# Neighbour-sum kernel: windowed one-hots in pass 1, and half of the spread moved to TensorE and ScalarE

## The chip, the cores and the metric

The kernel runs on one core of one Trainium2 chip. The metric is the device time in microseconds (us), as a median of several executions. Each experiment was timed in alternation with the kernel before on the same chip. On two of the five chips used for experiments the kernel before itself took about 477 us instead of 368, at a lower mean granted clock (0.81 to 0.85 instead of 0.91 to 0.93; the clock granted to TensorE, as a share of full speed); comparisons of totals from those two are marked as disturbed and carry no verdict.

## The reference

```python
# 4096 nodes x 128 f32 features, 65536 edges, random src and dst
output = zeros((4096, 128))
for i in range(65536):
    output[dst[i]] += node_features[src[i]]
```

## The kernel before

Work goes through 128-edge tiles (T = 512). **Pass 1** sorts edges by destination block (32 blocks of 128 nodes). It has six quads q0 to q5, each with four slices of up to 22 tiles. For each quad VectorE builds a one-hot of the block (`oh1s`: for every edge a row with a single 1), TensorE and ScalarE count ranks from it (`counts`, which starts from VectorE's `scan`, the running totals of the tiles), and VectorE multiplies that one-hot by two payloads (`spread1`: the code of the edge, and its source block plus one). For each slice VectorE then builds a one-hot of the rank over 128 slots, and TensorE moves the payloads into their slots (`move1`), giving `sa` and `sbk`. From those come the gather keys, and with them the indices of rows that GpSimd gathers for output blocks 0 to 7 from a bf16 copy of the features (three parts whose sum is the f32 value). **Pass 2** makes the 24 remaining output blocks (slots 0 to 23) from 32 small matrices each; the stretch in which pass 1 has ended and pass 2's first group is being prepared is called the transition here. TensorE writes into PSUM buffers; tiles that take turns in the same buffers are said to share a ring.

The letters V, S, G and PE stand for VectorE, ScalarE, GpSimd (POOL in the profile) and TensorE.

```python
    p2b = [sb1.tile([P, NCH, P], BF16, name=f"p2b{i}") for i in range(2)]
    for t in p2b:                                    # prologue fills
        G.memset(t[:, :NH, 64:], 0.0)
        G.memset(t[:, NH:, :64], 0.0)
    # ... cut ...
    def x_part(i, v):                                # part v of features, quarter i
        part = x3[:, i * BX:(i + 1) * BX, v, :]
        S.activation(out=part, in_=xf[i][:], func=COPY, scale=-1.0)
        if v < 2:
            for h in range(2):
                bs = slice(h * BX // 2, (h + 1) * BX // 2)
                G.tensor_tensor(out=xf[i][:, bs], in0=xf[i][:, bs], in1=part[:, bs], op=OP.add)
        # ... else: the quarter is written to x3d, from which rows are gathered ...

    def counts(q):
        # ... for every four tiles: early/sums matmuls into psc (ring psA), then
            S.activation(out=cum[...], func=RELU, bias=minus[:], in_=psc[...])
            yield
        # ... psr = sum of cum over blocks; rank1[q] = copy of psr ...

    def spread1(q):
        v1[q] = sb2.tile([P, NL, 2, NB], BF16, name="v1", tag="t1")
        for k, key in ((0, kab), (1, kb[:])):
            V.tensor_tensor(out=v1[q][:, :, k, :]..., in0=oh1q(q)..., in1=key[:, q, ...], op=OP.mult)

    def move1(q, meanwhile=lambda i: None):
        psm = ps.tile([P, 512], F32, name="psm", tag="misc", bufs=1)
        for l in range(4):
            # ... p1 for two slices, n tiles in this slice ...
            onehot(p1[:, l % 2, :n], rank1[q][:, l, :n], n)         # all 128 slots
            meanwhile(l)
            for j in range(n):
                PE.matmul(out=psm[:, l * 64:(l + 1) * 64], lhsT=p1[:, l % 2, j, :],
                          rhs=v1[q][:, 4 * j + l].rearrange("p k b -> p (k b)"), ...)
        S.copy(out=sa[:, place(q), :], ...)
        S.copy(out=sbk[:, place(q), :], ...)
    # ... cut ...
    for q in range(NQ):
        move1(q, during(q))                          # during: pieces of count(q + 2), x parts
        if q + 3 < NQ:
            oh1s(q + 3)
        if q + 1 < NQ:
            spread1(q + 1)
        if q == 1:
            serve(0)                                 # gather keys and gathers
        if 1 <= q < NQ - 1:
            serve(q)
        if q + 3 < NQ:
            scan(q + 3)
        # ... add_up: matmuls of gathered rows ...
```

## Time and profile before

| | before |
|---|---|
| median | 367.97 us (367.55 to 368.44) |
| profiled span, mean granted TensorE clock | 366.4 us, 0.921 |
| busy TensorE / VectorE / ScalarE / GpSimd | 299.4 / 287.0 / 160.2 / 224.5 us |
| first permutation one-hot of q0 starts | 19.41 us |
| copy of `sa` starts, q0 to q5 | 37.65, 45.97, 58.12, 68.89, 77.01, 86.98 us |
| first gather | 49.19 us |
| first result of pass 2, last result | 146.17 us, 363.08 us |

A line of the timeline has the start and the length in us, the engine, the source line, the operation, the output and input with their sizes, and how many instructions the group holds. A bracket at its end says how long the engine had been idle and what released it. The start of the `sa` copy is used below as the end E of a quad, since nothing that follows from the quad can begin earlier.

### The profile page before, as it was taken

To read this page: it belongs to the slowest core of one execution; us is meant where nothing else is said; L and a number is where in the kernel's file an instruction comes from. 1 tells how busy PE (TensorE), PEld (TensorE's weight loads), DVE (VectorE), ACT (ScalarE), POOL (GpSimd) and SP (SyncE) were. 2 spreads that over 40 slices of the span, in tenths; PEclk is the share of its full clock that TensorE was granted. 3 is DMA by queue.
4 is the path that set the end of the run, shared out by engine and by line. 5 is a ranking of instruction groups with operands and counts; after the bars stand their busy time and mean duration, and the time that the engine had idled before them with its cause. 6 is when DMAs were issued, how large, how long until landed. Compare 5 with 4: busy or idle time off the path is not lost.

```text
span 366.4 us, 8352 instructions
## 1 busy us (share of the span) xinstructions
PE 299.4 (82%) x3527; PEld 219.8 (60%) x3527; DVE 287.0 (78%) x476; ACT 160.2 (44%) x297; POOL 224.5 (61%) x225
## 2 busy tenths in 40 slices
PE   0768867656373597979989999997799999999996
PEld 0557746535351466756667767675477676767663
DVE  4982899999759689699994799659994959687721
ACT  2778733300000373525534553545345555464650
POOL 5677048787877777706887768578437575775000
PEclk9978988978565699989999999999899999999999
DMA  8400922233232233310324323232213332332000
GB/s 245 114 2 2 311 74 73 69 73 79 62 79 77 75 80 81 91 29 13 82 64 99 87 75 75 64 86 67 70 36 85 72 86 72 90 85 71 26 9 21
DMA packets 22694, 27.96 MB, mean 76 GB/s; under 512 B 3776, under 2 KB 19328, under 8 KB 22656
## 3 DMA queue, kind: packets, MB, share of 16 engines
q0 software_dynamic: 9216, 18.89, 21.2%
q1 hardware_dynamic: 13296, 8.01, 7.6%
q8 instruction: 27, 0.44, 0.5%
q10 hardware_dynamic: 144, 0.52, 0.4%
q14 instruction: 11, 0.09, 0.1%
HBM read 22.02 MB, written 5.39 MB: 75 GB/s over the span
## 4 chain that ended last, share of the span: by engine, by line
PE 55%; DVE 36%; ACT 5%; DMA 1%; issue 1%; DVEq 0%
PE pso L530 27%; DVE oh L196 10%; PE psa L524 9%; DVE p L196 8%; PE psg L325 6%; PE ps L496 4%; DVE cum L465 3%; DVE v L257 3%; DVE oh L442 3%; PE psr L474 3%; PE psb L449 2%; ACT cum L236 2%; DVE v L456 2%; PE psr L241 1%; ACT x L178 1%; DVE cum L470 1%
## 5 line engine op out<-in xcount | busy, mean ns | idle before, releaser
L306 POOL DMA_INDIRECT rows<-x3d,gidx x192 | 199.8, 1041 | 101.2 <-issue 48.1
L530 PE MATMUL pso<-x,a 128*128 128x384 bf16 x768 | 156.3, 328 | 5.5 <-DVE res L333 5.5
L526 ACT CAST a<-psa 128x512 bf16<-128x512 f32 x192 | 112.1, 586 | 77.5 <-PE psa L524 77.0
L530 PEld LDWEIGHTS <-a 128*128 128x128 bf16 x768 | 67.8, 98 | 32.1 <-issue 6.5
L524 PE MATMUL psa<-oh 128*128 128x128 bf16 x768 | 74.3, 220 | 1.2 <-ACT a L526 0.9
L524 PEld LDWEIGHTS <-oh 128*128 128x128 bf16 x768 | 59.0, 98 | 26.1 <-issue 2.5
L196 DVE TENSOR_TENSOR oh<-psi,slo 128x4096 bf16<-128x4096 uint16 x24 | 54.7, 2281 | 10.0 <-PE psa L524 10.0
L196 DVE TENSOR_TENSOR oh<-psi,dlo 128x4096 bf16<-128x4096 uint16 x24 | 54.7, 2278 | 0.0
L325 PE MATMUL psg<-rows,ohg 128*128 128x384 bf16 x192 | 40.2, 353 | 4.5 <-DMA rows<-x3d,gidx 3.0
L196 DVE TENSOR_TENSOR p<-psi,rank 128x2688 bf16<-128x2688 uint16 (+1 forms) x24 | 36.1, 1566 | 0.0
L325 PEld LDWEIGHTS <-ohg 128*128 128x128 bf16 x192 | 19.0, 104 | 17.1 <-DVE ohg L196 4.7
L504 DVE TENSOR_SCALAR slo<-pa 128x128 uint16<-128x128 uint16 x12 | 3.0, 252 | 32.8 <-ACT pa L500 32.8
L236 ACT ACTIVATE cum<-psc,minus 128x512 bf16<-128x512 f32 (+1 forms) x36 | 22.0, 656 | 12.2 <-PE psc L233 11.8
L182 POOL TENSOR_TENSOR xf<-xf,x 128x512 f32<-128x512 f32 x16 | 19.8, 1275 | 11.3 <-ACT x L178 11.3
L196 DVE TENSOR_TENSOR p2b<-psi,rank 128x768 bf16<-128x768 uint16 x48 | 23.3, 545 | 2.3 <-ACT rank L479 2.3
L280 PE MATMUL psm<-v,p 128*128 128x64 bf16 x512 | 20.6, 200 | 4.9 <-DVE p L196 4.8
L449 PE MATMUL psb<-oh,before 128*128 128x128 bf16 (+1 forms) x96 | 12.3, 309 | 14.7 <-DVE oh L442 11.8
L280 PEld LDWEIGHTS <-p 128*128 128x128 bf16 x512 | 18.6, 103 | 6.9 <-DVE p L196 6.5
L496 PEld LDWEIGHTS <-p2b 128*128 128x128 bf16 x576 | 19.7, 101 | 3.6 <-DVE p2b L196 2.1
L333 DVE TENSOR_REDUCE res<-pso 128x128 f32<-128x384 f32 x24 | 13.1, 546 | 10.0 <-PE pso L530 10.0
L233 PEld LDWEIGHTS <-sums 128*128 128x128 bf16 x126 | 12.1, 116 | 14.4 <-issue 6.6
L449 PEld LDWEIGHTS <-before 128*128 128x128 bf16 x96 | 10.0, 127 | 17.2 <-DVE oh L442 12.7
(72 smaller groups left out, 255.2 us busy)
## 6 DMA issues: line engine op xcount, KB each, us to landing
x3d<-x SPq DMA_DIRECT2D x4, 768.0 KB, 4.8
rows<-x3d,gidx POOLq DMA_INDIRECT x192
xf<-in_node_features_dram SPq DMA_DIRECT2D x4, 512.0 KB, 7.9
out_dram<-res SPq DMA_DIRECT2D x32, 64.0 KB, 1.9
raw<-in_edge_index_src_dram ACTq DMA_DIRECT2D x1, 512.0 KB, 5.2
raw<-in_edge_index_dst_dram SPq DMA_DIRECT2D x1, 512.0 KB
x3d<-zrow SPq DMA_DIRECT2D x1, 96.0 KB, 5.7
x3d<-zrow SPq DMA_DIRECT2D x1, 48.0 KB
```

The costliest lines, as they stand in the source:

```text
L182: G.tensor_tensor(out=xf[i][:, bs], in0=xf[i][:, bs], in1=part[:, bs], op=OP.add)
L196: V.tensor_tensor(out=dst.rearrange("p i (m k) -> p i m k", k=2), in0=io.rearrange("p i (m k) -> p i m k", k=2), in1=keys2[:, :, None, :]. ...
L236: S.activation(out=cum[:, :, 4 * j0:4 * (j0 + n)], func=RELU, bias=minus[:], in_=psc[:, :n * P].rearrange("p (t b) -> p b t", b=NB))
L280: PE.matmul(out=psm[:, l * 64:(l + 1) * 64], lhsT=p1[:, l % 2, j, :], rhs=v1[q][:, 4 * j + l].rearrange("p k b -> p (k b)"), start=j == 0, ...
L306: G.indirect_dma_start(out=t[:, l, :], out_offset=None, in_=x3d[:, :], in_offset=bass.IndirectOffsetOnAxis(ap=gidx[:, place(q).start + l, ...
L325: PE.matmul(out=psg[d][:, :3 * P], lhsT=oh[:, l, :], rhs=t[:, l, :], start=q == 0 and l == 0, stop=q == NQ - 1 and l == 3)
L333: V.tensor_reduce(out=res[:], in_=pso[:, :3 * P].rearrange("p (v f) -> p f v", v=3), op=OP.add, axis=AX.X, negate=True)
L449: PE.matmul(out=psb[:, h * W:(h + 1) * W], lhsT=before[:], rhs=flat2(oh2)[:, h * NH + c], start=c == 0, stop=c == NH - 1)
L496: PE.matmul(out=ps2[:, d % 2 * NB:(d % 2 + 1) * NB], lhsT=p2b[d % 2][:, c, :], rhs=v2[:, c, d // kk, :, d % kk], start=c == 0, stop=c == N ...
L524: PE.matmul(out=psa[:, i * P:(i + 1) * P], lhsT=oh[0][:, s, :], rhs=oh[1][:, s, :], start=True, stop=True)
L526: S.copy(out=a[:, k * 4:k * 4 + 4, :], in_=psa[:].rearrange("p (s m) -> p s m", s=4))
L530: PE.matmul(out=pso[:, :3 * P], lhsT=a[:, s, :], rhs=x3[:, s, :, :].rearrange("p v f -> p (v f)"), start=s == 0, stop=s == NB - 1)
```

## The change

The intent is to take work from VectorE, which is full in q1 to q5. (1) An edge's rank grows with its tile, so with random edges early tiles use low slots, and late ones high slots: a slice becomes three windows (`WIN`), and the rest of the one-hot tile is filled with zeros once. An edge outside its window would be lost, so the final check now also counts the edges that arrived. (2) The source-block half of the spread of q1 to q5 becomes sums on TensorE, 4096 times the one-hot plus the key, and a ReLU with bias -4096 on ScalarE. (3) To make room on ScalarE, eight of twelve conversions of the features go to GpSimd, issued right after the prologue. (4) Scan and code spread move in among the slices. (5) The steps of pass 2 are regrouped, and the final check is made cheaper.

```diff
+WIN = ((0, 7, 0, 64), (7, 14, 4, 100), (14, NJ, 20, P))
+    p1 = [sb1.tile([P, 2, NJ, P], BF16, name=f"p1{i}", tag=f"t2{i}") for i in range(2)]
+    for t in p1:
+        for j0, j1, m0, m1 in WIN:
+            if m0 > 0:
+                G.memset(t[:, :, j0:j1, :m0], 0.0)
+            if m1 < P:
+                G.memset(t[:, :, j0:j1, m1:], 0.0)
     def x_part(i, v):
-        S.activation(out=part, in_=xf[i][:], func=COPY, scale=-1.0)
+        if v == 0:
+            S.activation(out=part, in_=xf[i][:], func=COPY, scale=-1.0)
+        else:
+            G.tensor_single_scalar(out=part, in_=xf[i][:], scalar=-1.0, op=OP.mult)
+    def spread_blocks(q):
+        for t0 in range(0, NL, 16):
+            ...
+            psv = ps.tile([P, 512], F32, name="psv", tag="psA")
+            PE.matmul(out=psv[:, :n], lhsT=large[:], rhs=oh1q(q)[...], start=True, stop=False)
+            PE.matmul(out=psv[:, :n], lhsT=identb[:], rhs=kb[...].to_broadcast(...), ..., stop=True)
+            S.activation(out=v1[q][:, ts, 1, :], in_=psv[...], func=RELU, bias=minus[:])
+            yield
     def move1(q, meanwhile=lambda i: None):
-            onehot(p1[:, l % 2, :n], rank1[q][:, l, :n], n)
+            for j0, j1, m0, m1 in WIN:
+                j1 = min(j1, n)
+                onehot(t[:, l % 2, j0:j1, m0:m1], rank1[q][:, l, j0:j1], j1 - j0, m1 - m0, m0=m0)
     # between the slices l of quad q
+            if q + 1 < NQ:
+                if l == 0:
+                    spread1(q + 1, ks=(0,))
+                    parts = spread_blocks(q + 1)
+                for _ in range(2 if l in (0, 3) else 1):
+                    next(parts, None)
+                if l == 1 and q > 0:
+                    scan(q + 2)
     # after the slices
-        if q + 1 < NQ:
-            spread1(q + 1)
-        if q + 3 < NQ:
-            scan(q + 3)
     # ... cut: pass 2's steps as lists (buckets and psb, payloads, ...), slot 0's blocks ahead of
     # group 1's psb; the final check with one reduction ...
```

## The prediction

> **What bounds the kernel now.** I first read the chain that ended last: TensorE holds 55% of it and VectorE 36%, but those are averages over stages with different limits.
>
> ```profile
> PE 55%; DVE 36%; ACT 5%; DMA 1%; issue 1%; DVEq 0%
> ```
>
> So I next read busy time by stage, with windows cut where the VectorE timeline begins each of the six quads q0 to q5 of pass 1 (columns: stretch, its length, then busy time and instruction count per engine, clock, DMA).
>
> ```profile
> 19.00:37.60 18.60, 14.25 (x240) 11.56 (x236) 10.90 (x8) 14.93 (x26) 13.65 (x12) 0.82 0.04 14
> 37.60:49.30 11.70, 7.63 (x170) 6.19 (x169) 11.67 (x15) 6.68 (x15) 0.11 (x1) 1.00 0.81 251
> 49.30:60.60 11.30, 8.43 (x165) 7.07 (x165) 11.04 (x13) 4.52 (x10) 9.17 (x8) 0.85 0.25 63
> 60.60:70.20 9.60, 7.76 (x142) 6.49 (x142) 9.59 (x12) 4.52 (x10) 7.47 (x8) 0.83 0.31 75
> ```
>
> The third busy figure is VectorE: full in q1, q2, q3 (and q4: 9.99 of 10.00 us), but not in q0, where it waits 7.4 us for a count behind ScalarE and TensorE. One full quad on VectorE, in order of time:
>
> ```profile
> 49.30 5.92 DVE L196 TENSOR_TENSOR p<-psi,rank 128x2688 bf16<-128x2688 uint16 x4
> 55.15 1.61 DVE L196 TENSOR_TENSOR oh<-psi,kd 128x2816 bf16<-128x2816 uint16 x1
> 56.68 1.61 DVE L257 TENSOR_TENSOR v<-oh,ka 128x2816 bf16<-128x2816 bf16 x1
> 58.21 1.61 DVE L257 TENSOR_TENSOR v<-oh,kb 128x2816 bf16<-128x2816 bf16 x1
> ```
>
> The change shortens the first row and removes the last. Beside it TensorE and ScalarE finish a quad like this:
>
> ```profile
> 66.83 1.41 PE L241 MATMUL psr<-cum,identb 128*128 128x88 bf16 x32 [0.28 <-ACT cum L236]
> 68.04 0.69 PEld L280 LDWEIGHTS <-p 128*128 128x128 bf16 x21
> 68.08 0.78 PE L280 MATMUL psm<-v,p 128*128 128x64 bf16 x21
> 68.28 0.40 ACT L245 CAST rank<-psr 128x88 bf16<-128x88 f32 x2 [1.50 <-PE psr L241]
> ...
> 68.89 0.27 ACT L284 CAST sa<-psm 128x128 bf16<-128x128 f32 x1 [0.22 <-PE psm L280]
> 69.06 0.27 ACT L285 CAST sbk<-psm 128x128 bf16<-128x128 f32 x1
> ```
>
> Ranks are summed, the last slice is moved, and its result (sa, sbk) is copied; only now can the gather keys be made. Let E be the end of that last psm group: 37.05, 45.93, 58.1, 68.86, 76.97 and 86.95 us for q0 to q5 (group start plus length, or the sa copy's start). Pass 1 ends at 86.95.
>
> The waits also show the largest TensorE gap, 9.4 us, between the passes. There VectorE waits too:
>
> ```profile
> 122.67 1.76 DVE L456 TENSOR_TENSOR v<-oh,sa 128x3072 bf16<-128x3072 bf16 x1
> 124.35 0.74 DVE L196 TENSOR_TENSOR ohg<-psi,gkey 128x512 bf16<-128x512 uint16 x2
> 129.47 2.29 DVE L196 TENSOR_TENSOR oh<-psi,slo 128x4096 bf16<-128x4096 uint16 x1 [4.38 <-PE psa L524]
> ```
>
> From about 142 us TensorE is busy 91 to 96% of the stage: a shift of its start moves the end, little else does.
>
> **What the Trainium skill says.** "GPSIMD Engine Reference", 1. Specifications: its SBUF interfaces are shared with VectorE, and contention comes from VectorE instructions with two SBUF inputs or in a two-port mode. The trace agrees: the spread (two SBUF inputs) took 1.91 and 2.57 us while GpSimd subtracted, 1.61 later, but four one-hots (one input in PSUM) took 6.19 us both beside GpSimd at 19.4 and without it at 37.7. The same page, 4.1 Engine selection, calls one-input work on GpSimd roughly line rate; a one-input multiply there is not in this trace, the memsets took 0.68 us for 768 elements start to start. "ScalarE: Activation LUTs", What ACT_TABLE_LOAD costs: a [128,1] pointer operand adds about 93 ns to an ACTIVATE. Agrees: 0.69 us for a single ReLU with pointer bias against 0.59 for the 128x512 cast. So a new ReLU piece is 0.69, less back to back.
>
> **The change, part by part.**
> *One-hots.* Three windows instead of one. Start-to-start times (2.20 us for 4096 elements, 0.465 for 768) give 66 ns plus 0.521 ns per element. Elements: 448+672+864=1984 for 22 columns, 1876 for 21. A slice falls from 1.53 to about 1.23, or 1.465 to 1.175; 24 slices save 7 us of VectorE.
> *Block spread.* Five of six leave VectorE: 5 x 1.53 = 7.7 us. TensorE gains 60 matmuls (per quad about 5.5 x 2 x 0.21 = 2.4 us), ScalarE 6 ReLU pieces per quad, 3.3 us, both through the same two PSUM buffers (psA) that counting uses.
> *Copies of x.* Eight conversions leave ScalarE (about 8 x 1.0 us) for GpSimd. From about 24.6 us it has 4 x (2 x 1.0 + 2.24) = 17 us: done near 42, written near 47. Gathers start at 49.19 today, so this is hidden.
> *New order in pass 1.* In the built program the code spread of q+1 comes after slice 0 of q, and the scan for q+2 after slice 1. Keys of q now stand directly ahead of q+1's first one-hot. Before, two spreads (3.07 us) filled the wait for sbk; now VectorE stands there. If VectorE alone were the bound, q2 would take 4.7+1.53+1.53+0.4+0.1 = 8.3 us instead of 11.3. It is not, by this path for q2 and q3, measured from E of the quad before:
> - sa, sbk and keys: 0.95. Slice 0: 1.18. Spread: 1.53. Slice 1: 1.18. Scan with its latency: 0.19. Sum 5.03: only now can counting start.
> - After it, ScalarE has 6 counting pieces (3.6) and 3 spread pieces (1.4) in one alternating queue with TensorE; with a first matmul (0.35) and about 1.25 of stalls where a psm group (0.68) holds TensorE while both buffers drain: 6.6.
> - psr 1.24, last psm group 0.8. Total about 13.7.
>
> For q1 the keys of q0 come early; the spread waits for its buffer (E of q0), the scan is ready at 3.0: 3.0+6.7+2.1 = 11.75. q4 has no counting: keys 0.95, ohg 0.33, slices 4.7, spread 1.53, psm 0.8 = 8.3. q5: 0.95+0.66+4.7+0.8 = 7.1. For q0 ScalarE loses four x copies and gains six pieces, so it stays near 37 (36 to 37.5).
> Sum: 37+11.75+13.7+13.7+8.3+7.1 = 91.5, against 86.95: pass 1 becomes **4.6 us longer**, though VectorE lost 15 us.
> *Between the passes.* The step lists are regrouped: slot 0's blocks now stand ahead of group 1's psb on TensorE. They can run at about 114.5 (old clock), when their one-hots are ready, instead of behind the buckets at 125.2. The 4.38 us wait of VectorE goes. Two gather keys also move into the 2.95 us wait for pa: 0.66. **5.1 us saved**, and VectorE is the chain there, so it reaches pass 2.
> *Flag.* Six reductions become one, near the end, off the path: 0.
>
> **The sum.** 368.0 + 4.6 - 5.1 = 367.5. I put the middle at 366.5, since the stalls of 1.25 us per quad are my choice and could be smaller.
>
> **Rivals.**
> (1) VectorE remains the bound of q1 to q5. Then q1 starts near 28.5 and pass 1 ends near 66: about 342 us. For it: VectorE is full there today, and VectorE work shrank most. Against: the scan, keys and buffer waits above, and TensorE and ScalarE would have to run 12 handovers in 8.3 us.
> (2) TensorE's clock: it read 0.82 to 0.85 in q0, q2, q3, and counting matmuls took 0.63 instead of 0.38 in spells. More pauses could add 1 us a quad: 371. Against: TensorE gets more work there.
> (3) GpSimd's copies are slower (two-input speed, contention with spreads) and gathers start past 52 us. Gather sums first wait near 80, so it costs 0 to 3 us.
> (4) Gather supply limits the transition. The sums there had about 4 us of slack at 110.6, and gathers should start slightly earlier. Unlikely.
>
> **Range and chances.** Errors in pass 1 of -5 to +4 us and in the transition of +-1.5 give 360 to 371.5. Faster by over 2% means below 360.6, which needs quads near 11 us: 0.13. Slower by over 2% means above 375.3: 0.04. Within: 0.83.
>
> **What would show it.** Right: VectorE one-hot groups of three windows near 1.2 us per slice, no block spread after q0, yet VectorE waiting at the keys and the scan; E-to-E near 12 to 14 us for q1 to q3; pass 1 ending near 91; slot 0's blocks before psb, and no 4.4 us wait of VectorE there. Wrong: E-to-E under 10 us (then far faster, rival 1), a slow clock in pass 1, gathers starting after 52 us, or a pass 2 whose length from slot 2 on changes by over 2 us.

## The result

The changed kernel takes 373.17 us (median of 4, 372.45 to 373.65), and the kernel before 367.96 in the same rounds. The ratio is 1.0139, with a 95% interval of 1.0119 to 1.0160. Ratios here are the mean time of one kernel's fast runs over that of the other's of the same rounds, so they are not quite the ratio of the medians. That is within the 2% that was given the greatest chance, but the time lies 1.7 us above the range's upper end: the prediction of the time was wrong.

| start, us | before | after | shift |
|---|---|---|---|
| first permutation one-hot of q0 | 19.41 | 22.45 | +3.04 |
| E of q0 | 37.65 | 41.57 | +3.92 |
| E of q1 | 45.97 | 53.91 | +7.94 |
| E of q2 | 58.12 | 68.36 | +10.24 |
| E of q3 | 68.89 | 81.99 | +13.10 |
| E of q4 | 77.01 | 90.17 | +13.16 |
| E of q5 | 86.98 | 96.76 | +9.78 |
| VectorE's one-hots of slot 2 | 129.47 | 133.08 | +3.61 |
| 1st, 13th, 14th, 24th result of pass 2 | 146.17, 274.78, 285.87, 363.08 | 149.77, 278.49, 290.91, 368.25 | +3.60, +3.71, +5.04, +5.17 |

These times, like all that are read from traces below, come from one profiled execution of each kernel. So 3 us were lost before the first permutation one-hot, almost 10 by the end of pass 1, 6.2 came back in the transition, and 1.3 were lost again between two results of pass 2. The chain that ended last in the profile of after:

```profile
PE 60%; DVE 29%; ACT 5%; DMA 2%; issue 2%; POOL 1%; DVEq 0%
```

VectorE's share of that chain fell by seven points (from 36%), as intended, and TensorE's rose by five. Busy time by stage, cut at the E of each quad (columns: stretch, length, TensorE, weight loads, VectorE, ScalarE, GpSimd with instruction counts, granted clock, DMA share, GB/s):

```profile
22.50:41.60 19.10, 15.95 (x228) 11.72 (x226) 9.90 (x19) 13.17 (x25) 18.14 (x11) 0.82 0.13 42
41.60:53.90 12.30, 9.80 (x186) 7.25 (x183) 8.62 (x15) 8.08 (x16) 12.04 (x6) 1.00 0.22 68
53.90:68.40 14.50, 10.24 (x185) 7.24 (x183) 9.12 (x18) 8.15 (x17) 9.11 (x5) 1.00 0.35 110
68.40:82.00 13.60, 9.97 (x174) 7.08 (x170) 6.77 (x17) 8.08 (x17) 10.47 (x11) 1.00 0.27 68
```

VectorE is full nowhere any more: in q3 it works 6.77 of 13.60 us. Only GpSimd is nearly full, in q0 and q1. One quad of VectorE after shows why:

```profile
68.66 0.17 DVE L331 TENSOR_SCALAR gslo<-sa 128x32 uint16<-128x32 uint16 x1 [5.33 <-ACT sa L320]
...
69.05 1.25 DVE L215 TENSOR_TENSOR p<-psi,rank 128x448 bf16<-128x448 uint16 x3
70.22 1.61 DVE L277 TENSOR_TENSOR v<-oh,ka 128x2816 bf16<-128x2816 bf16 x1
71.75 1.25 DVE L215 TENSOR_TENSOR p<-psi,rank 128x448 bf16<-128x448 uint16 x3
72.92 0.19 DVE L239 TENSOR_TENSOR_SCAN sums<-ones,pst 128x22 bf16<-128x22 bf16 x1
73.03 2.40 DVE L215 TENSOR_TENSOR p<-psi,rank 128x448 bf16<-128x448 uint16 x6
82.29 0.36 DVE L331 TENSOR_SCALAR gslo<-sa 128x32 uint16<-128x32 uint16 x1 [6.86 <-ACT sa L320]
```

VectorE ends the slices at 75.4 us and then stands for 6.86 us at the gather keys, which need the `sa` of the quad. That `sa` waits for the last slice, whose matmuls stand behind the counting of the quad after next on TensorE. ScalarE in the same quad:

```profile
73.61 1.27 ACT L255 ACTIVATE cum<-psc,minus 128x512 bf16<-128x512 f32 x2 [1.72 <-PE psc L252]
...
81.99 0.27 ACT L320 CAST sa<-psm 128x128 bf16<-128x128 f32 x1 [0.22 <-PE psm L316]
```

ScalarE's first counting piece starts at 73.61 us, 5.25 us after the E before (68.36), once the scan at 72.92 has run; the prediction put the start of counting at 5.03. The prologue, VectorE before and then after:

```profile
5.90 0.57 DVE L157 TENSOR_SCALAR kd<-raw 128x176 uint16<-128x176 uint16 x3 [2.88 <-DMA raw<-in_edge_index_dst_dram]
...
8.38 0.71 DVE L165 SCALAR_TENSOR_TENSOR raw<-raw 128x528 uint16<-128x528 uint16 x1
```

```profile
6.15 2.28 DVE L173 TENSOR_SCALAR kd<-raw 128x176 uint16<-128x176 uint16 x3 [3.09 <-DMA raw<-in_edge_index_dst_dram]
...
10.58 1.54 DVE L181 SCALAR_TENSOR_TENSOR raw<-raw 128x528 uint16<-128x528 uint16 x1
```

The three first keys take four times as long, and the combined shift-and-or (second line) twice, though the instructions are unchanged. GpSimd's last fill before, and its last fill and first feature additions after:

```profile
4.95 0.73 POOL L141 MEMSET p2b<- 128x768 bf16 x1
```

```profile
8.27 0.83 POOL L157 MEMSET p2b<- 128x768 bf16 x1
9.10 2.45 POOL L201 TENSOR_TENSOR xf<-xf,x 128x512 f32<-128x512 f32 x2
```

With eight more fills GpSimd still writes until 9.1 us, over the time in which VectorE makes its first keys. Each of the three keys ends 0.1 us after one of the fills (fills at 6.77, 7.55 and 8.33 us, keys at 6.87, 7.65 and 8.43). The shift-and-or doesn't meet the fills: it runs from 10.58 to 12.12 us, beside the feature additions, which before began at 9.03 us, when it was all but done. So of the 3.0 us the keys lost 1.7 beside the fills; 1.1 more went to the shift-and-or and the instruction ahead of it (0.66 us instead of 0.42), which came late and so ran beside the additions; the indices landed 0.25 us later. GpSimd later in pass 1, after, and its first gather before:

```profile
42.21 6.76 POOL L197 TENSOR_SCALAR x<-xf 128x1024 bf16<-128x1024 f32 x2
...
60.41 2.77 POOL L197 TENSOR_SCALAR x<-xf 128x1024 bf16<-128x1024 f32 x1
68.49 1.17 POOL L342 DMA_INDIRECT rows<-x3d,gidx  x1 [5.31 <-issue]
```

```profile
49.19 1.10 POOL L306 DMA_INDIRECT rows<-x3d,gidx  x1 [12.40 <-DVE gkey L296]
```

A conversion takes 2.77 us (one of the eight 4.02) rather than the 1.0 that was estimated, and the first gather comes 19 us later. In the transition TensorE now makes slot 0's blocks at 123.63 us, ahead of group 1's `psb`, and VectorE's wait ahead of the third pair of one-hots is gone:

```profile
132.41 0.74 DVE L215 TENSOR_TENSOR ohg<-psi,gkey 128x512 bf16<-128x512 uint16 x2
133.08 2.27 DVE L215 TENSOR_TENSOR oh<-psi,slo 128x4096 bf16<-128x4096 uint16 x1
```

The last loss stands in pass 2. In both kernels TensorE waits 5 us there for a result to be taken from PSUM (5.0 before, 5.1 after). The stretch of 5 us behind that wait, before and after (clock is the third figure from the end):

```profile
260.00:265.00 5.00, 5.00 (x40) 3.34 (x39) 5.00 (x3) 2.35 (x4) 1.89 (x2) 0.81 0.29 71
```

```profile
264.00:269.00 5.00, 5.00 (x27) 3.05 (x25) 5.00 (x3) 1.76 (x3) 3.50 (x4) 0.53 0.32 79
```

After, the granted clock stays low for nearly the whole stretch, and 27 matmuls are recorded instead of 40. In narrower windows it reads 0.50 from 258.5 to 261.9 us before, so for 3.4 us, and from 261.9 to 268.7 us after, for 6.8 us. From the 13th to the 14th result the kernel before needed 11.09 us, the changed one 12.42.

### The profile page after: what moved, and what is told of

The parts are those of the page before. It is cut to its first block, busy times and chain, and to the rows that moved or that the text cites. A ratio compares the mean times of both kernels' runs of the same rounds, so it can differ in the third digit from the quotient of the medians.

```text
span 371.6 us, 8563 instructions
## 1 busy us (share of the span) xinstructions
PE 311.9 (84%) x3588; PEld 224.2 (60%) x3588; DVE 278.1 (75%) x515; ACT 171.6 (46%) x319; POOL 255.4 (69%) x242
## 4 chain that ended last, share of the span: by engine, by line
PE 60%; DVE 29%; ACT 5%; DMA 2%; issue 2%; POOL 1%; DVEq 0%
PE pso L577 27%; DVE oh L215 9%; PE psa L571 9%; PE psg L361 5%; PE ps L540 4%; DVE p L215 3%; DVE cum L510 3%; DVE oh L487 3%; PE psm L316 3%; PE psr L260 3%; DVE v L502 2%; PE psc L248 2%; PE psr L519 2%; DVE v L277 2%; ACT v L293 2%; PE psc L252 2%
## 5 line engine op out<-in xcount | busy, mean ns | idle before, releaser
L571 PEld LDWEIGHTS <-oh 128*128 128x128 bf16 x768 | 60.7, 101 | 27.0 <-issue 2.7
L571 PE MATMUL psa<-oh 128*128 128x128 bf16 x768 | 76.4, 224 | 0.7 <-ACT a L573 0.7
L361 PE MATMUL psg<-rows,ohg 128*128 128x384 bf16 x192 | 38.8, 340 | 5.3 <-DVE ohg L215 2.7
L215 DVE TENSOR_TENSOR p<-psi,rank 128x448 bf16<-128x448 uint16 (+3 forms) x72 | 29.6, 476 | 2.9 <-ACT cum L255 2.9
L201 POOL TENSOR_TENSOR xf<-xf,x 128x512 f32<-128x512 f32 x16 | 22.1, 1404 | 8.3 <-ACT x L195 8.0
L293 ACT ACTIVATE v<-psv,minus 128x512 bf16<-128x512 f32 (+1 forms) x30 | 18.6, 650 | 11.7 <-PE psv L290 8.3
L197 POOL TENSOR_SCALAR x<-xf 128x1024 bf16<-128x1024 f32 x8 | 23.3, 2928 | 0.4
L252 PEld LDWEIGHTS <-sums 128*128 128x128 bf16 x126 | 10.9, 106 | 18.2 <-issue 9.3
```

Source lines behind the costliest of these rows:

```text
L197: G.tensor_single_scalar(out=part, in_=xf[i][:], scalar=-1.0, op=OP.mult)
L215: V.tensor_tensor(out=dst.rearrange("p i (m k) -> p i m k", k=2), in0=io.rearrange("p i (m k) -> p i m k", k=2), in1=keys2[:, :, None, :]. ...
L293: S.activation(out=v1[q][:, ts, 1, :], in_=psv[:, :n].rearrange("p (t b) -> p t b", b=NB), func=RELU, bias=minus[:])
L361: PE.matmul(out=psg[d][:, :3 * P], lhsT=oh[:, l, :], rhs=t[:, l, :], start=q == 0 and l == 0, stop=q == NQ - 1 and l == 3)
L571: PE.matmul(out=psa[:, i * P:(i + 1) * P], lhsT=oh[0][:, s, :], rhs=oh[1][:, s, :], start=True, stop=True)
```

## The experiments

All but the last block of this section build on the changed kernel or on the kernel before with one or a few parts put back. "Rows waits" are TensorE's waits for gathered rows from 85 to 150 us. All gave a correct result.

### 1. Fills on VectorE (e1_zeros_vector)

```diff
-                G.memset(t[:, :, j0:j1, :m0], 0.0)      # the same for m1:
+                V.memset(t[:, :, j0:j1, :m0], 0.0)
```

> The changed kernel (373.2 us) with the eight zero fills of the permutation tiles on VectorE, in its idle time before the indices land, instead of on GpSimd. Theory A (the fills keep GpSimd busy until 9.1 us and slow VectorE's first key instructions, 2.28 us instead of 0.57 for three): the first one-hot of pass 1 starts near 19.4 us instead of 22.45 and the whole gets about 3.0 us faster, near 370.2. Rival (the start is late for another reason, the landing of the indices or the new constant): no change, 373.

Measured: 369.74 us, 1.0026 of before (0.9989 to 1.0064), against 1.0139 for the changed kernel. The first keys take 0.57 us again and the first permutation one-hot starts at 19.18 us:

```profile
5.76 0.57 DVE L173 TENSOR_SCALAR kd<-raw 128x176 uint16<-128x176 uint16 x3 [0.88 <-DMA raw<-in_edge_index_dst_dram]
```

The two intervals don't meet: moving the fills was worth 3.4 us by the medians and 4.2 by the ratios. E of q0 is 36.25 us, inside the 36 to 37.5 of the prediction, and pass 1 ends at 92.16 where 91.5 was predicted. That q0 fits so well is in part luck with the clock. In the changed kernel it read 0.50 from 26.4 to 33.2 us, in the kernel before from 23.0 to 29.8, but through e1's q0 it was 1.00. ScalarE's copy of the ranks of q1 waits for TensorE's sum of the ranks (`psr`), in the changed kernel and then in e1:

```profile
30.50 0.39 ACT L264 CAST rank<-psr 128x88 bf16<-128x88 f32 x2 [2.59 <-PE psr L260]
```

```profile
26.00 0.39 ACT L264 CAST rank<-psr 128x88 bf16<-128x88 f32 x2 [1.50 <-PE psr L260]
```

From the first permutation one-hot to E, q0 took 18.24 us before, 19.12 after and 17.07 in e1. In m2 (section 9), which also fills on VectorE but had 6.8 us of the low clock in q0, it took 19.23, and E of q0 was 38.41: 3.2 us ahead of the changed kernel, not 5.3. (m2 differs in its order and its copies too.) In e1 the first result of pass 2 stands at 146.06 us against 146.17 before: with this one thing mended, the gains and losses of the change cancel. The later 1.6 us (last result 364.63 against 363.08) come mostly from the low clock between the 13th and the 14th result, 12.19 us here too.

### 2. The other way round: fills doubled in the kernel before (k2_fills_twice)

```diff
-    for t in p2b:
+    for t in p2b + p2b:
         G.memset(t[:, :NH, 64:], 0.0)
         G.memset(t[:, NH:, :64], 0.0)
```

> The kernel before with its four zero fills on GpSimd done twice, 2.7 us more of GpSimd before 8.5 us and nothing else. Theory A (a busy GpSimd slows VectorE's key instructions at 6 us): the first permutation one-hot starts 2 to 3 us later than 19.4 and the whole is 2 to 3 us slower, near 371. Rival: the fills are hidden, 368 to 369.

This fell on a disturbed chip (before 476.58 us there), so the total, 479.06 us and 1.0083 (1.0000 to 1.0165), decides nothing. Up to 25 us the trace can be read all the same, next to that of k1 below, which ran on the same chip with the usual fills:

```profile
5.75 2.27 DVE L157 TENSOR_SCALAR kd<-raw 128x176 uint16<-128x176 uint16 x3 [2.73 <-DMA raw<-in_edge_index_dst_dram]
```

```profile
5.82 0.57 DVE L157 TENSOR_SCALAR kd<-raw 128x176 uint16<-128x176 uint16 x3 [2.80 <-DMA raw<-in_edge_index_dst_dram]
```

The first is with doubled fills, the second without. The permutation one-hot started at 21.84 against 19.34 us. Four fills of no use are enough for the loss of 2.5 us; the cause is shown from both sides. (The start alone would not show it on such a chip: in g1 and c1b of section 11, whose first keys took 0.57 us, it came at 21.63 and 21.84 us, behind a `psr` of 2.51 us. In k1 and k2 `psr` took the same 1.41 us, and VectorE is 2.9 us late already when it starts the source-block key, after the shift-and-or: 11.85 against 8.93 us.)

### 3. Scan and spread in an earlier order (e2_order)

```diff
     # between the slices l of quad q
-                if l == 0: spread1(q + 1, ks=(0,)) ...       # code spread after slice 0
-                if l == 1 and q > 0: scan(q + 2)
+                if l == 0 and q > 0: scan(q + 2)
+                if l == 3: spread1(q + 1, ks=(0,))
     # gather keys of quad q: not at its end but after slice 1 of quad q + 1
```

> The changed kernel with VectorE's order alone altered: the scan for q+2 directly after slice 0, the code spread after slice 3, the gather keys after slice 1 of the next quad, so that VectorE holds up nobody. Theory B (half of the longer quads is VectorE's order: keys, spread and scan stand ahead of the counting): the ends of q1, q2, q3 follow at about 11.5 us each instead of 12.4, 14.4, 13.6, and the whole gets 4 to 5 us faster, near 368.5. Rival (the alternating TensorE and ScalarE queue is the bound by itself): at most 1.5 us faster, 372.

Measured: 374.44 us (370.52 to 375.20), 1.012 (1.005 to 1.019): no gain, a miss. Yet q1 to q3 did what was expected: 11.96, 11.84 and 11.84 us, E of q3 at 76.14 instead of 81.99 (pass 1 ends at 93.44 instead of 96.76; TensorE already waits 3.8 us for rows between 80 and 94 us). The waits of TensorE in the transition show where it went:

```profile
PE psg L362 <- DMA rows<-x3d,gidx: 11.4, 13, 1.3
```

(Total, times, longest.) In the changed kernel these waits were 2.6 us in 3. The gathers start at 69.22 us, and what pass 1 gained was spent waiting for rows. So the order of keys, scan and spread on VectorE, which e2 moved together, makes up about 1.8 us of a quad of 13.6 and 2.6 of one of 14.5, but mending it alone is worth nothing.

### 4. Both spreads on VectorE (e4_spread_vector)

```diff
-    # spread_blocks on TensorE and ScalarE, scan among the slices
+        if q + 1 < NQ: spread1(q + 1)                # after the slices, as before
+        if q + 3 < NQ: scan(q + 3)
```

> The changed kernel with both spreads back on VectorE at their old places (windows, GpSimd copies and step lists kept). Theory D (the spread through TensorE and ScalarE made pass 1 longer): q5 ends near 83 us instead of 96.7; but gathers still start near 67, and the tenth group lands near 119, so the transition then waits for rows: 364 to 368. Rival (VectorE is the bound of pass 1): q5 ends later than 97 and the whole is slower, 378 or more.

Measured: 375.02 us, 1.0152 (1.0114 to 1.0190). Another miss by the same wall: E of q3 at 69.71, 12 us earlier than in the changed kernel, gathers at 70.62, and waits for rows of 11.7 us in 15. They begin in pass 1 itself (9.4 us from 60 to 93 us), which so ends at 93.16 and not near 83.

### 5. Conversions on ScalarE (e3_x_scalar)

```diff
-            G.tensor_single_scalar(out=part, in_=xf[i][:], scalar=-1.0, op=OP.mult)
+            S.activation(out=part, in_=xf[i][:], func=COPY, scale=-1.0)   # issued as before
```

> The changed kernel with the eight conversions of x back on ScalarE at their old places. Theory C (late gathers cost little, but ScalarE in q0 and q1 is full): gathers start near 52 us instead of 68.5, yet q0 and q1 end 3 to 5 us later, so 374 to 378. Rival (the late start of the gathers, 2.75 us a conversion on GpSimd, holds the transition): pass 2 starts earlier, 369 to 371.

Measured: 374.36 us, 1.0137 (1.0097 to 1.0176), so as slow as the changed kernel. Gathers come at 55.89 us and no wait for rows is left, but E of q0 moves to 45.09 and pass 1 ends at 100.05 us: on ScalarE the conversions stand in the way of counting and spreading.

### 6. Conversions on GpSimd in the kernel before (b2_gpsimd_copies)

```diff
     # in the kernel before, x_part(i, 1) and x_part(i, 2) right after the prologue, on
-        S.activation(out=part, in_=xf[i][:], func=COPY, scale=-1.0)
+        G.tensor_single_scalar(out=part, in_=xf[i][:], scalar=-1.0, op=OP.mult)   # v > 0
```

> The kernel before with the eight x conversions on GpSimd and nothing else. Theory (2.75 us each, so gathers start near 65 us and become the bound of the first sums): q0 ends 3 to 4 us earlier, but TensorE waits over 8 us for rows before slot 0 and the whole is 3 to 8 us slower, 371 to 376. Rival (the late start is hidden as I predicted): 364 to 366.

Measured: 377.07 us, 1.022 (1.0191 to 1.0250). Gathers start at 65.16 us, and TensorE waits 7.6 us for rows. It is slower than before, though whether by 2% stays unclear; of the parts tried alone in the kernel before, it loses most.

### 7. Which form is slow on GpSimd (k1_copy_forms, then m1_plain_copies)

k1 is b2 with a plain copy for the second part and an addition for the third. Its output is wrong, which doesn't matter for the time. The sum of the three parts changes only in its last digits, and the check of results still passed.

```diff
-            G.tensor_single_scalar(out=part, in_=xf[i][:], scalar=-1.0, op=OP.mult)
+            if v == 1: G.tensor_copy(out=part, in_=xf[i][:])
+            else:      G.tensor_tensor(out=part[:, bs], in0=xf[i][:, bs], in1=xf[i][:, bs], op=OP.add)
```

> Wrong result on purpose: the kernel before with GpSimd conversions, the second part of x as a plain copy and the third as two-input adds of 512 elements, to see what a GpSimd conversion costs by its form. Theory (any one-input conversion of 1024 elements is slow there): copies near 2.75 us, two adds near 2.3 us. Rival (the multiply by a constant is slow): copies near 1.0 us.

On the disturbed chip (482.10 us) a plain copy of the 128x1024 tile took 1.04 us (one of the four 2.43), against 2.77 us for the multiply in the changed kernel, and gathers started at 56.71 us. m1 makes this correct and in the changed kernel: all three parts stay positive, and the final sum is not negated.

```diff
-            G.tensor_single_scalar(out=part, in_=xf[i][:], scalar=-1.0, op=OP.mult)
+            G.tensor_copy(out=part, in_=xf[i][:])
-                G.tensor_tensor(out=xf..., in0=xf..., in1=part..., op=OP.add)
+                G.tensor_tensor(out=xf..., in0=xf..., in1=part..., op=OP.subtract)
-            V.tensor_reduce(..., op=OP.add, axis=AX.X, negate=True)
+            V.tensor_reduce(..., op=OP.add, axis=AX.X)
```

> The changed kernel with the three feature parts kept positive, so that GpSimd converts with a plain copy and a subtraction in place of a multiply by -1 and an addition (the minus sign is also dropped at the end; the result stays correct). Theory (the multiply by a constant is GpSimd's slow form, 2.75 us against 1.04 us for the copy of the same tile): eight conversions save about 14 us, GpSimd is done near 47 to 50 us and the first gather starts near 50 to 55 us rather than at 68.5 us; the waits for gathered rows in the transition vanish. The total moves little, 371 to 373 us, because pass 1 still ends at 96.8 us. Rival (GpSimd is slowed mainly by VectorE on the shared port): the copies take 2 us or more here too, and the gathers start after 62 us.

```profile
28.99 1.04 POOL L197 CAST x<-xf 128x1024 bf16<-128x1024 f32 x1
...
53.87 1.12 POOL L342 DMA_INDIRECT rows<-x3d,gidx  x1 [5.68 <-issue]
```

Measured: 371.52 us, 1.0113 (1.0071 to 1.0155); the rival is out, for seven of the eight copies took 1.04 us and only one 2.44: the form was the cause. Pass 1 still ends at 96.37 us, so the first result of pass 2 comes only 0.9 us earlier (148.87 against 149.77), and the last 2.0 us earlier, because the clock recovered sooner here (11.11 us from the 13th to the 14th result, 3.4 us of it at 0.50). The late gathers cost the changed kernel about 1 us; in faster pass 1s they cost all the gain.

### 8. The parts that gain, alone (b1_slots, c1_windows_slots)

b1 is the kernel before with the regrouped step lists and the cheaper check. c1 adds the windows, with their fills on VectorE. Neither has the spread on TensorE or the conversions on GpSimd.

```diff
     # both against the changed kernel; b1
-WIN = ((0, 7, 0, 64), (7, 14, 4, 100), (14, NJ, 20, P))
+WIN = ((0, NJ, 0, P),)
     # b1 and c1: x_part on ScalarE, spread1 on VectorE; c1: windows kept, V.memset
```

> The kernel before with the regrouped step lists (and the shorter flag) alone: no windows, both spreads on VectorE, x on ScalarE. Theory: slot 0's blocks run ahead of group 1's psb, VectorE's 4.4 us wait and 0.66 us of keys go, so 5 us faster, near 363. Rival (what slot 0 gives up is taken back by a later wait): 366 or more.

> The same with the three windows, zero fills on VectorE: VectorE saves 0.3 us per slice and is the bound of q1 to q5 there. Theory: about 5 us faster than the step lists alone, near 358, with q5 ending near 81 us. Rival (gather supply is the next wall): rows are waited for and less than 2 us of it shows, 361 or more.

Measured on one chip, with before at 369.02: b1 362.75 us, 0.9851 (0.9812 to 0.9891), and c1 **356.86 us, 0.9687 (0.9655 to 0.9720)**. In b1 pass 1 ends as before (86.90 us) and the first result comes at 139.32 instead of 146.17: the step lists alone are worth 6.9 us in the transition. In c1 pass 1 ends at 80.66, 6.2 us earlier: the windows were worth about what the prediction computed for VectorE (7), as long as VectorE bounds the quads. c1 beats both kernels by more than any other version here, and it is the only one whose whole interval lies more than 2% under before.

### 9. All mended, with the spread on TensorE and ScalarE (f_order_early, m2_all_mended)

f has the fills on VectorE, the earlier order and the conversions on ScalarE; m2 has plain copies on GpSimd instead of the last.

```diff
     # f = changed kernel + edits of 1, 3 and
-            G.tensor_single_scalar(out=part, in_=xf[i][:], scalar=-1.0, op=OP.mult)
+            S.activation(out=part, in_=xf[i][:], func=COPY, scale=-1.0)  # issued as in before
     # m2 = changed kernel + edits of 1, 3 and m1
```

> The changed kernel with VectorE's better order, zero fills on VectorE and x on ScalarE, so that gathers start near 52 us: only the spread through TensorE and ScalarE sets it apart from windows plus step lists. Theory (the alternating queue still takes 11.5 to 12 us a quad and ScalarE also holds the x copies in q0 and q1): no waits for rows, q5 near 91 us, 364 to 367. Rival (without late gathers and with the order mended the spread pays): 358 or less.

> The changed kernel with all three mends: fills on VectorE, scan and spread in the earlier order, plain copies on GpSimd; the TensorE and ScalarE spread stays. Theory (the loss is prologue fills, then the hand-over at each quad, then late gathers, and nothing else): pass 1 ends near 86 to 88 us, no wait for rows, total 359 to 363 us against about 368.5 before, so a clear gain of 1.5 to 2.5 per cent. Rival (the TensorE and ScalarE spread itself makes pass 1 longer whatever the order): quads near 11.8 us and pass 1 near 86.5 us as with the conversions on ScalarE, total 363 us or more.

Measured: f 363.21 us, 0.9868 (0.9827 to 0.9908), on the chip of c1; m2 358.97 us, 0.9758 (0.9714 to 0.9803), on another. In m2 pass 1 ends at 85.13 us, the gathers start at 52.92 and only 1.4 us of row waits remain. m2 has the order of e2 with fills and copies mended, and there the order pays: an estimate for fills and copies without it is 368.1 us (371.52 of m1 less the 3.4 of e1). The rival of m2 is half right: quads stay at 11.96, 11.84 and 11.84 us in m2 (12.43, 11.84 and 11.84 in f), while c1's are 8.05, 10.75 and 8.20 with the spread on VectorE. On the chip of c1, with the conversions on ScalarE, the spread on VectorE is the faster by 6.4 us (356.86 against f's 363.21). With plain copies on GpSimd, m3 of section 11, on the chip of m2, has it on VectorE and takes 358.20 us against 358.97, equal within the noise. So these runs don't show that one place is the better for the spread in general; here it went with where the conversions run.

### 10. A ring of its own for the spread (h1_two_rings, h1b_two_rings)

```diff
     # on top of f
-            psv = ps.tile([P, 512], F32, name="psv", tag="psA")
+            psv = ps.tile([P, 512], F32, name="psv", tag="psg" if q < NQ - 1 else "psA")
```

> The version with the mended order and early gathers (363.2 us), its spread sums now in the two PSUM buffers that are idle until the first gather sum, so that spread and counting no longer share two buffers (q1 to q4). Theory (hand-over stalls in the shared pair are a part of the 11.8 us a quad): 10.8 us or less each for q2 and q3, 2 to 3 us faster, near 360.5. Rival (the work of TensorE and ScalarE itself fills the quad): 11.8 us again, 363.

> A repeat, on another chip, of the run that fell on a disturbed one: the changed kernel with fills on VectorE, the earlier order and the conversions on ScalarE, and the spread's PSUM tiles taken from another ring than the ranks'. Theory that sharing one pair of PSUM banks between spread and ranks is part of the 11.8 us a quad: quads of 11 us or less, total 360 to 362 us. Rival (the chain of one-hots, matmuls and ScalarE itself): quads stay at 11.8 us, total 363 us within 1 us.

h1 fell on a disturbed chip: 475.45 us, 0.9937 (0.9824 to 1.0051), inconclusive. Its repeat h1b: 360.42 us, 0.9826 (0.9781 to 0.9871). The quads are 11.08, 10.36 and 10.35 us, so about 1.5 us of 11.8 was the PSUM pair that spread and counting share. ScalarE in q2, f and then h1b:

```profile
59.04 1.05 ACT L291 ACTIVATE v<-psv,minus 128x512 bf16<-128x512 f32 x2 [0.36 <-PE psv L288]
60.42 1.05 ACT L252 ACTIVATE cum<-psc,minus 128x512 bf16<-128x512 f32 x2 [0.32 <-PE psc L249]
```

```profile
57.56 1.05 ACT L291 ACTIVATE v<-psv,minus 128x512 bf16<-128x512 f32 x2
58.51 1.05 ACT L252 ACTIVATE cum<-psc,minus 128x512 bf16<-128x512 f32 x2
```

The waits in brackets are gone. Pass 1 ends 3.5 us earlier than in f (83.10 against 86.56), and the first result 2.7 us earlier (136.82 against 139.47), with 3.2 us of row waits in between. The gain is read from the quads: the totals of f and h1b, on two chips, have intervals that overlap.

### 11. Attempts at a still better version (m3, g1, m4, c1b)

m3 is c1 with the plain copies on GpSimd. g1 is c1 with only the last quad's spread on TensorE and ScalarE. m4 is m2 with h1's ring. c1b repeats c1 beside m4.

```diff
     # m3, on top of c1
-            S.activation(out=part, in_=xf[i][:], func=COPY, scale=-1.0)    # v > 0
+            G.tensor_copy(out=part, in_=xf[i][:])
     # g1, on top of c1, among the slices of q4
+                    late.append(spread_blocks(q + 1))
     # m4, on top of m2
-            psv = ps.tile([P, 512], F32, name="psv", tag="psA")
+            psv = ps.tile([P, 512], F32, name="psv", tag="psg" if q < NQ - 1 else "psA")
     # c1b: c1 without an edit
```

> The windows and the step lists of the change with fills and both spreads on VectorE, and the conversions of the second and third part as plain copies on GpSimd. The version with the same conversions on ScalarE ran in 356.9 us. Theory (GpSimd at 1.04 us a copy is fast enough and frees ScalarE): gathers from 50 to 55 us, pass 1 ends at 80 to 81 us, total 354 to 357 us. Rival (copies and subtractions on GpSimd slow VectorE, or come too late): pass 1 ends after 82 us or gathers after 60 us, total over 358 us.

> Windows and step lists with VectorE's spread (356.9 us), the block spread of the last quad alone through TensorE and ScalarE, in q4, where nothing is counted. Theory (VectorE bounds q4 and both engines are idle there): 1.5 us faster, near 355.4. Rival (rows are already waited for, 1.7 us, before slot 0): no gain, 356.9.

> The changed kernel with all mends together: fills on VectorE, earlier order, plain copies on GpSimd, and the spread's PSUM tiles in their own ring. The version without the ring ran in 358.97 us, 0.976 of before. Theory (the mended parts add up and the spread on TensorE and ScalarE is then no longer a loss): quads near 10.4 us, pass 1 ends near 82 us, total 355.5 to 358 us. Rival (the gathers, which start near 53 us, are the next wall): pass 1 ends earlier but waits for rows of 3 us or more take it back, total 358 us or more.

> A repeat on this chip of the windows and step lists with fills and spreads on VectorE and conversions on ScalarE, 356.86 us and 0.969 of before on another chip, to compare it directly. Theory (the spread is worth as much on VectorE as on the other two engines once the rest is mended): within 1 per cent of the mended changed kernel. Rival (the VectorE spread is the better one): 0.967 to 0.972 of before, and over 1 per cent faster than the other.

m3: 358.20 us, 0.9785 (0.9722 to 0.9848), not better than c1, a miss; E of q0 falls to 33.11 us, but q2 then takes 15.5 us and pass 1 ends at 80.60, where it ended. In q2 TensorE waits 6.3 us for the scan, which stands behind both spreads on VectorE. g1, m4 and c1b fell on disturbed chips: g1 473.55 us, 0.9940 (0.9876 to 1.0004); m4 471.81, 0.9893 (0.9847 to 0.9939); c1b 472.50, 0.9878 (0.9829 to 0.9927). m4 and c1b are equal beside each other there, with clocks of 0.865 and 0.834, but what is equal on that chip need not be on an undisturbed one. Whether m4 reaches c1 stays open.

## Why the prediction was wrong, point by point

**Right: the path that sets q1 to q5.** From E to E the quads took 12.34, 14.45, 13.63, 8.18 and 6.59 us; 11.75, 13.7, 13.7, 8.3 and 7.1 were predicted, a sum of 55.2 against 54.55. VectorE stands at keys and scan as described, and e2 shows that moving keys, scan and spread shortens the quads. Sharing the buffers, for whose stalls 1.25 us a quad had been set, cost 1.5 us a quad in f, as h1b shows. Rival 1, VectorE as the bound, did not come. Rival 2, the clock, did not come in pass 1: it was 1.00 in q1 to q5, and in q0 0.82 as before.

**Wrong: the step "it stays near 37 (36 to 37.5)" for q0.** It was 41.57 us. The prediction counted what ScalarE loses and gains in q0, and gave no cost at all to the eight new fills on GpSimd in the prologue, although it cited the shared interfaces of the two engines for the spread. 3.0 us were lost ahead of the first permutation one-hot. e1 puts that one-hot back to 19.18 and the whole kernel 3.4 us down; k2 makes the loss appear in the kernel before. This is the term that failed. The rest of the 4.6 us was mis-sized: from the first permutation one-hot to E the prediction implied 17.6 us (19.41 to 37), and it took 19.12, longer than the 18.24 before, with 6.8 us at a clock of 0.50 in both. At a clock of 1.00 it took 17.07, in e1.

**Mis-sized, with little cost: "4 x (2 x 1.0 + 2.24) = 17 us: done near 42 ... this is hidden".** The multiply took 2.77 us instead of 1.0, and the gathers began at 68.49. Rival 3 had put 0 to 3 us on that; m1 shows 0.9 us at the first result. The 1.0 was right for a plain copy (1.04 us). Rival 4, gather supply, was called unlikely; it was not the bound of the changed kernel but became that of e2 and e4.

**Mis-sized in the other direction: "5.1 us saved" between the passes.** The shift fell from 9.78 to 3.61 us, so 6.2; b1 alone shows 6.9.

**Not foreseen: a longer spell of low clock in pass 2, 1.3 us.** From the 13th to the 14th result the changed kernel, e1, h1b and m3 needed 12.2 to 12.4 us, f and b2 11.6 and 11.9, but before, m1, m2 and c1 only 11.1 to 11.2. The first six had the clock at 0.50 for 6.8 us there, the last four for 3.4. No run was made to control it, so what decides between the two stays open.

The sum with the measured terms, from the 367.5 of the text: +4.6 for q0 (41.57 for 37), +0.6 for the other quads, -1.1 for the transition and +1.3 for the clock give 372.9; 373.17 was measured. Without the fills' 3.0 us it would have been near 370, inside the range, which e1's 369.74 confirms. The choice of 366.5 in place of the 367.5 had rested on stalls in the quads being smaller than assumed; they were not. Some of the prediction's sums are off a little: 4.38 + 0.66 is 5.04 and not 5.1, 5.5 x 2 x 0.21 is 2.3 and not 2.4, and its errors of +4 and +1.5 reach 372.0 from 366.5 and not 371.5. None of this changes the outcome.

## What to carry to other kernels

When work is moved onto an engine that looks idle, write down what that engine shares with the busy one at that very moment: here eight cheap fills cost 3 us because they held up VectorE's first keys, which then also ran beside GpSimd's additions, and doing them on VectorE in the time it waited for its input cost nothing. Time a form of instruction before counting on it: negating by multiply made a conversion 2.7 times as long as a plain copy. And when a mend frees one stage and the total doesn't move, look for the supply behind it before judging it: the order that was worth nothing by itself was in the version that ran 2.4% under before, once fills and copies were mended too.

## What the Trainium skill lacked or had wrong

- "GPSIMD Engine Reference", 4.1 Engine selection, calls one-input work roughly line rate. For a 128x1024 tile from f32 to bf16 that fits the plain copy (1.04 us) but not the multiply by a constant (2.77 us); the section has no figure for either.
- "VectorE: DVE Perf Modes", the perf-mode tier table, has `tensor_tensor` with any PSUM operand at 1x, at a clock of 0.96 GHz. The one-hots here, with one uint16 input in PSUM, took 2.20 us start to start for 4096 elements, 1.9 elements per ns, which is twice that. The page's own section "Why PSUM operands drop a tier" limits to 1x only fp32 and lets other types reach double rate, which fits: it is the table's row that is too low.
